# Fewer block pairs at the end of an up projection, and each pair's last product issued one product later

## Chip, cores and metric

The kernel runs on one core of a Trainium2 chip. The metric is the device time of one execution in microseconds (us), lower is better; the time of a kernel is the median of its runs.

## What is computed

Two residual layers on 512 tokens of width 1024, in float32. Each has a token mixer, a cross attention into 256 memory tokens, and a squared-ReLU MLP, every sub-layer followed by a layer norm. The change lies in the MLP, which is run twice, once in each layer:

```python
def sq_relu_mlp(x, w1, b1, w2, b2):          # x 512x1024, w1 1024x4096, w2 4096x1024
    return jnp.square(jax.nn.relu(x @ w1 + b1)) @ w2 + b2
...
x = layer_norm(ALPHA * x + sq_relu_mlp(x, mlp_w1[i], mlp_b1[i], mlp_w2[i], mlp_b2[i]),
               ln_g[i, 2], ln_b[i, 2])
```

## The kernel before

**Number format.** Every float32 operand is split into a high part h and a low part l of a type that TensorE takes at full rate: ScalarE (ACT) casts the high part, VectorE (DVE) subtracts it from the raw value for the low part. A product is then three matmuls: h by h, l by h, h by l (`mm3`, lines 198 to 200 are its three matmuls). So each 128x1024 tile of weights costs one ScalarE cast and one VectorE subtraction before TensorE may read it. The split weights lie in two pools of five buffers each, `wh` and `wl`; a buffer is free again when its last matmul has run.

**The MLP.** The 4096 hidden features are worked in four quarters q of 1024, eight tiles of 128 features each. Quarters 0 to 2 go through `up_down`, quarter 3 through plain products. In `up_down` the up projection makes the hidden values `s`, two buffers of four tiles; the down projection then multiplies them by the quarter of w2 with Strassen's scheme, seven block products (`product`, 24 matmuls of 512 columns each) instead of eight.

**The up projection** takes the eight tiles in four pairs, m = 0, 2, 4, 6. A plain pair is two calls of `feat_tile`, 24 matmuls of 512 columns each, and an evacuation `ev` by ScalarE (Relu and Square, lines 915 and 916). A block pair (`up_pair`) is seven products of 12 matmuls of 256 columns: its VectorE forms sums of weight blocks (lines 869 to 873, buffers of pool `rawd`, six of them), four splits follow (`ub`, `utb`, `uta` of 1024 columns, `ud` of 512; lines 864 and 865), and the seven products are added up by evacuations on both engines (lines 888 to 900). The first, second and the last product belong to `ub`, `ub` and `utb`; the last is `prod(pa, t4, block(1, 1), False)`, copied at line 900 and followed by Relu and Square of both tiles (lines 902 and 903). Which pairs are block pairs stands in `STRASSEN_UP`: none in quarter 0, pairs 1, 2, 3 of quarter 1, all four of quarter 2.

**The start of the down projection.** The first product, into the PSUM banks `u`, needs block a11 of `s` (split by `first_blocks`, line 778 and 779, as soon as the first four tiles are there) and block b11 of w2 (`weight_split`, lines 787 and 788, two halves). The second product, into `f`, needs

- t1, a sum of weight blocks. It is made in place: once b11 is split, GpSimd (POOL) issues a DMA that adds another block of w2 onto the same buffer (`onto_w`, line 968, one per half), and the sum is then split, `t101h` and `t101l` in quarter 1 of layer 0;
- q1, the split of a21 - a22 (line 974, then lines 778 and 779, `q101h`), for which all eight tiles must be done.

A third block sum, t3, is made in the same way from buffers `t`.

**Order.** A planner decides the order of the instructions on each engine before the kernel runs. It goes by program order, but lets a later instruction go ahead of an earlier one when, by its own estimate of durations, the earlier is not ready. On the chip each engine then runs its list in that order, and waits at whatever comes next.

Of the kernel before, what the change touches and what calls it, by code (L numbers as in the profile page):

```python
# [11 lines left out]
AF = mybir.ActivationFunctionType  # L12
# [21 lines left out]
SUM = sum(SEG)  # L34
WU = 1024
LN_T = 7.2
STRASSEN_UP = ((), (1, 2, 3), (0, 1, 2, 3))


def f32(ap):  # L40
    return ap.bitcast(F32)
# [3 lines left out]
def trunk(ctx: ExitStack, tc: tile.TileContext, a: dict, out: bass.AP):  # L45
    nc = tc.nc
    V, A, G, T = nc.vector, nc.scalar, nc.gpsimd, nc.tensor
# [43 lines left out]
    def ld(dst, src):  # L91
        nc.sync.dma_start(dst, src)

    def const_tile(name, shape):
        t = const.tile(shape, F32, name=name)
        ld(t, a[name])
        return t
# [83 lines left out]
    def chain(us, step, fns):  # L181
        for n, fn in enumerate(fns):
            defer(us + step * n, fn)
# [32 lines left out]
    def hf_cols(hf):  # L216
        return slice(hf * 512, (hf + 1) * 512)
# [266 lines left out]
    b1 = const_tile("b1", [P, DEPTH, DFF // P])  # L484
# [169 lines left out]
    for i in range(DEPTH):  # L654
# [147 lines left out]
        def block(r, c):  # L802

            return xm.half(c, slice(256 * r, 256 * r + 256))

        def x_sums():
# [42 lines left out]

            chain(3, 5, [start, q3, q1, q2, q4, end])  # L850

        def up_pair(q, m, n, s):


            src = [a["w1"][i, 8 * q + m + z] for z in range(2)]
            h2 = slice(0, 512), slice(512, 1024)
            u1, u2 = [raw_p.tile([P, WU], F32, tag="raw", name=f"up{n}{m + z}") for z in range(2)]
            ld(u1, src[0])
            ld(u2, src[1])
            ta, tb = [scoped["rawd"].tile([P, WU], F32, tag="rawd", name=f"ut{n}{m}{z}") for z in "ab"]  # L860

            def hl(name, r):
                h, l = [p.tile([P, WU], F32R, tag=t, name=f"{name}{n}{m}{t}")[:, : r.shape[1]] for p, t in ((wh_p, "wh"), (wl_p, "wl"))]
                A.copy(h, r)
                V.tensor_tensor(l, r, f32(h), ALU.subtract)
                return [tuple(z[:, c].rearrange("p (k m) -> p k m", m=P) for z in (h, l)) for c in h2[: r.shape[1] // 512]]

            b11, b21 = hl("ub", u1)
            V.tensor_tensor(ta[:, h2[0]], u1[:, h2[0]], u2[:, h2[0]], ALU.add)
            V.tensor_tensor(tb[:, h2[0]], ta[:, h2[0]], u2[:, h2[1]], ALU.add)  # L870
            V.tensor_tensor(tb[:, h2[1]], tb[:, h2[0]], u1[:, h2[1]], ALU.add)
            t2_, t4 = hl("utb", tb)
            V.tensor_tensor(ta[:, h2[1]], u2[:, h2[0]], u2[:, h2[1]], ALU.add)
            t1, t3 = hl("uta", ta)
            (b22,) = hl("ud", u2[:, h2[1]])

            pa = acc_p.tile([P, 512], F32, tag="acc", name=f"ua{n}{m}")[:, :256]
            pb = acc_p.tile([P, 512], F32, tag="acc", name=f"ub{n}{m}")[:, :256]
            pc = aux_p.tile([P, 512], F32, tag="aux", name=f"uc{n}{m}")[:, :256]
            z1, z2 = s[:, m % 4], s[:, m % 4 + 1]  # L880
            lo, hi = slice(0, 256), slice(256, 512)

            def prod(ps, w, x_, start):
                for k in range(4):
                    mm3(ps, (w[0][:, k], w[1][:, k]), (x_[0][:, k], x_[1][:, k]), start=start and k == 0, stop=k == 3, skip=not start)

            prod(pa, b11, block(0, 0), True)
            A.copy(z1[:, lo], pa)
            prod(pc, b21, block(0, 1), True)
            V.tensor_tensor(z1[:, lo], z1[:, lo], pc, ALU.add)  # L890
            prod(pa, t2_, xq["q2"], False)
            A.activation(z2[:, lo], pa, AF.Copy, scale=-1.0)
            prod(pb, t1, xq["q1"], True)
            A.copy(z2[:, hi], pb)
            prod(pa, t3, xq["q3"], False)
            V.tensor_tensor(z2[:, hi], z2[:, hi], pa, ALU.subtract)
            prod(pb, b22, xq["q4"], False)
            V.tensor_tensor(z2[:, lo], z2[:, lo], pb, ALU.add)  # L898
            prod(pa, t4, block(1, 1), False)
            A.copy(z1[:, hi], pa)  # L900
            for c, z in enumerate((z1, z2)):
                A.activation(z, z, AF.Relu, bias=b1[:, i, 8 * q + m + c : 8 * q + m + c + 1], scale=1.0)  # L902
                A.activation(z, z, AF.Square)

        def up_down(q, n):

            s = [act_p.tile([P, 4, S], F32, tag="act", name=f"s{n}{b}") for b in range(2)]

            def ev(m, ps):
                r = t2(f"r{n}{m}")
                A.activation(r, ps, AF.Relu, bias=b1[:, i, 8 * q + m : 8 * q + m + 1], scale=1.0)
                A.activation(s[m // 4][:, m % 4], r, AF.Square)

            first = 0
            if q == 0:
                feat_first(f"h{n}", 4, lambda m: a["w1"][i, m], xm, ev)  # L920
                first = 4
                assert not later
                b2 = raw_p.tile([P, D], F32, tag="raw", name=f"b2{i}")
                ld(b2, a["b2"][i : i + 1, :].broadcast_to([P, D]))
                for t in range(NT):
                    V.scalar_tensor_tensor(x[t], x[t], ALPHA, b2, ALU.mult, ALU.add)
            a11, a21 = s[0][:, :, :256], s[0][:, :, 256:]
            a12, a22 = s[1][:, :, :256], s[1][:, :, 256:]
            L, R = {}, {}

            def load(name, hf, j):
                z = [scoped["rawd"].tile([P, WU], F32, tag="rawd", name=f"{name}{n}{z}") for z in range(2)]
                for w in range(2):
                    ld(z[w], a["w2"][i, q, hf, j + w])
                return z

            def first_blocks():
                L["M1"] = split(f"a11{n}", a11)
                V.tensor_tensor(a11, a11, a21, ALU.subtract)
                L["M7"] = split(f"q3{n}", a11)  # L940

            if q == 0:
                first_blocks()
                x_sums()
            for m in range(first, KC, 2):
                if m // 2 in STRASSEN_UP[q]:
                    up_pair(q, m, n, s[m // 4])
                else:
                    for z in range(2):
                        ev(m + z, feat_tile(f"h{n}{m + z}", a["w1"][i, 8 * q + m + z], xm, aux_p, "aux"))  # L950
                if m == 2:
                    first_blocks()

            def onto(row, hf, op=ALU.add):
                def evac(g, ps):
                    z = x[2 * row + g][:, hf_cols(hf)]
                    V.tensor_tensor(z, z, ps, op)

                return evac

            def banks(name, p, tag):
                return [p.tile([P, 512], F32, tag=tag, name=f"{name}{n}{g}") for g in range(2)]

            u, f, m2 = banks("u", acc_p, "acc"), banks("f", acc_p, "acc"), banks("m2", tmp_p, "tmp")
            def onto_w(z, hf, j):

                for w in range(2):
                    G.dma_start(z[w], a["w2"][i, q, hf, j + w], accum_op=ALU.add)  # L968

            b = load("b11", 0, 0)  # L970
            w = weight_split(f"b11{n}", b)
            onto_w(b, 1, 0)
            product(u, L["M1"], w, True, onto(0, 0))
            V.tensor_tensor(a21, a21, a22, ALU.subtract)
            w = weight_split(f"t1{n}", b)
            onto_w(b, 1, 2)
            product(f, split(f"q1{n}", a21), w, True, onto(1, 1))
            b21 = load("b21", 0, 2)
            l12 = split(f"a12{n}", a12)
            product(m2, l12, weight_split(f"b21{n}", b21), True, onto(0, 0))  # L980
            t3 = load("t3", 1, 0)
            onto_w(t3, 1, 2)
            V.scalar_tensor_tensor(a11, a11, -1.0, a22, ALU.mult, ALU.subtract)
            w = weight_split(f"t2{n}", b)
            onto_w(b, 0, 2)
            product(u, split(f"q2{n}", a11), w, False, onto(0, 1, ALU.subtract))
            product(u, L["M7"], weight_split(f"t3{n}", t3), False, onto(1, 1, ALU.subtract))
            b22 = load("b22", 1, 2)
            V.tensor_tensor(a12, a12, a11, ALU.add)
            product(f, split(f"q4{n}", a12), weight_split(f"b22{n}", b22), False, onto(0, 1))  # L990
            product(u, split(f"a22{n}", a22), weight_split(f"t4{n}", b), False, onto(1, 0))
# [113 lines left out]
```

## Time and profile before

| | us |
|---|---|
| median of 3 runs | 1243.29 |
| lowest to highest run | 1242.1 to 1243.35 |
| profiled execution, its own time | 1241.42 |
| its span, first to last instruction | 1239.7 |
| TensorE busy | 1191.8 (96%) |
| VectorE busy | 857.7 (69%) |
| ScalarE busy | 617.9 (50%) |

The span is that of the profiled execution, from the first to the last instruction; the time of that execution is 1.7 us longer. A busy share of 96% leaves some 48 us in which TensorE had no matmul running. The granted clock of TensorE is 0.981 of full speed on average. The page of the profile has the span in 40 slices; to find where the idle time lies one asks the trace for TensorE's waits, and then for the order of time around each.

### The profile page before, as it was taken

The numbers are of one execution on the slowest core, as the hardware profiler recorded it, in microseconds if no ns is written. First come the engines' busy times: TensorE is split into PE (matmuls) and PEld (weight loads), VectorE is DVE, ScalarE is ACT, GpSimd is POOL, SyncE is SP. The second block draws the span as 40 slices with busy tenths as digits, with TensorE's granted clock in tenths as the row PEclk, the third lists the DMA queues.
The fourth block names the chain that finished last, engine by engine and source line by source line (L and its number), as shares of the span: only waits on it lengthen the run. The fifth ranks groups of instructions, "written<-read, shape, count | busy, mean of one in ns | idle before, by whom it ended". The sixth has DMA issues, their size and how long they took to land.

```text
span 1239.7 us, 16808 instructions
## 1 busy us (share of the span) xinstructions
PE 1191.8 (96%) x6609; PEld 1035.7 (84%) x6609; DVE 857.7 (69%) x1191; ACT 617.9 (50%) x924; POOL 62.1 (5%) x99
## 2 busy tenths in 40 slices
PE   9999999999999999799799999999999979979997
PEld 7888898898889789689688889988988968968886
DVE  6673575575567996597585599866889659758336
ACT  6585864135324646446446443652464554644430
POOL 0221000000000100100100000000010010010000
PEclk9999999999999999899899999999999989989999
DMA  8253258433255535835745455626453482583411
GB/s 277 77 143 108 86 189 294 146 103 102 82 156 154 102 85 168 172 68 175 165 114 194 127 185 195 192 86 186 139 117 79 158 175 65 181 177 85 119 52 68
DMA packets 50976, 171.85 MB, mean 139 GB/s; under 512 B 6336, under 2 KB 6604, under 8 KB 50896
## 3 DMA queue, kind: packets, MB, share of 16 engines
q1 hardware_dynamic: 42960, 142.96, 35.8%
q0 software_dynamic: 7936, 27.81, 12.5%
q8 instruction: 52, 0.85, 0.3%
q14 instruction: 28, 0.23, 0.1%
HBM read 164.43 MB, written 6.31 MB: 138 GB/s over the span
## 4 chain that ended last, share of the span: by engine, by line
PE 79%; DVE 9%; DMA 5%; ACT 4%; issue 2%; SPq 0%; DVEq 0%; ACTq 0%
PE h L198 5%; PE h L199 5%; PE h L200 5%; PE m L199 3%; PE m L198 3%; PE m L200 3%; DMA b<-in_w 3%; PE u L198 2%; PE u L199 2%; PE u L200 2%; PE ao L198 2%; PE ao L200 2%; PE ao L199 2%; PE q L198 2%; PE q L199 2%; PE q L200 2%
## 5 line engine op out<-in xcount | busy, mean ns | idle before, releaser
L162 DVE TENSOR_TENSOR wl<-raw,wh 128x1024 fp32r<-128x1024 f32 x147 | 179.1, 1220 | 145.9 <-ACT wh L161 143.9
L161 ACT CAST wh<-raw 128x1024 fp32r<-128x1024 f32 x147 | 153.7, 1049 | 226.3 <-PE h L199 52.4
L968 POOL DMA_DIRECT2D b<-in_w x36 | 31.7, 882 | 282.4 <-DVE b1100l L788 62.7
L968 POOL DMA_DIRECT2D t<-in_w x12 | 11.5, 996 | 680.0 <-DMA t<-in_w 451.2
L249 ACT ACTIVATE rs<-mv,eps_t 128x1 f32<-128x1 f32 x24 | 7.1, 295 | 53.2 <-DVE mv L247 53.2
L198 PE MATMUL h<-xm10h,wh 128*128 128x512 f32 (+1 forms) x88 | 31.0, 352 | 0.0
L198 PE MATMUL h<-xm00h,wh 128*128 128x512 f32 (+1 forms) x88 | 31.0, 352 | 0.0
L198 PE MATMUL h<-xm01h,wh 128*128 128x512 f32 (+1 forms) x88 | 31.0, 352 | 0.0
L198 PE MATMUL h<-xm11h,wh 128*128 128x512 f32 (+1 forms) x88 | 31.0, 352 | 0.0
L199 PE MATMUL h<-xm00l,wh 128*128 128x512 f32 (+1 forms) x88 | 30.9, 352 | 0.0
L199 PE MATMUL h<-xm10l,wh 128*128 128x512 f32 (+1 forms) x88 | 30.9, 351 | 0.0
L200 PE MATMUL h<-xm00h,wl 128*128 128x512 f32 (+1 forms) x88 | 30.8, 350 | 0.0
L200 PE MATMUL h<-xm01h,wl 128*128 128x512 f32 (+1 forms) x88 | 30.8, 350 | 0.0
L200 PE MATMUL h<-xm10h,wl 128*128 128x512 f32 (+1 forms) x88 | 30.8, 350 | 0.0
L200 PE MATMUL h<-xm11h,wl 128*128 128x512 f32 (+1 forms) x88 | 30.8, 350 | 0.0
L199 PE MATMUL h<-xm01l,wh 128*128 128x512 f32 (+1 forms) x88 | 30.8, 350 | 0.0
L199 PE MATMUL h<-xm11l,wh 128*128 128x512 f32 (+1 forms) x88 | 30.8, 350 | 0.0
L677 ACT ACTIVATE pr<-s,nm 128x256 f32<-128x256 f32 x32 | 14.9, 471 | 10.4 <-DVE nm L672 7.6
L902 ACT ACTIVATE s<-s,b 128x512 f32<-128x512 f32 x28 | 18.9, 718 | 2.0 <-DVE s L898 2.0
L199 PEld LDWEIGHTS h<-xm10l,wh 128*128 128x128 f32 x88 | 16.7, 189 | 2.3
L199 PEld LDWEIGHTS h<-xm00l,wh 128*128 128x128 f32 x88 | 16.7, 189 | 2.2
L198 PEld LDWEIGHTS h<-xm00h,wh 128*128 128x128 f32 x88 | 16.7, 189 | 2.2
(1696 smaller groups left out, 4259.3 us busy)
## 6 DMA issues: line engine op xcount, KB each, us to landing
raw<-in_w SPq DMA_DIRECT2D x60, 512.0 KB, 3.8
b<-in_w SPq DMA_DIRECT2D x36, 512.0 KB, 4.5
b<-in_w POOLq DMA_DIRECT2D x36, 512.0 KB, 5.7
up<-in_w SPq DMA_DIRECT2D x28, 512.0 KB, 3.7
raw<-in_w_q SPq DMA_DIRECT2D x24, 512.0 KB, 4.1
raw<-in_w_ao SPq DMA_DIRECT2D x16, 512.0 KB, 3.7
t<-in_w SPq DMA_DIRECT2D x12, 512.0 KB, 3.8
t<-in_w POOLq DMA_DIRECT2D x12, 512.0 KB, 9.8
```

Of the source, the lines that this page charges most:

```text
L161: A.copy(h, r)
L162: V.tensor_tensor(l, r, f32(h), ALU.subtract)
L198: T.matmul(out_, l[0], r[0], start=start, stop=False, skip_group_check=skip)
L199: T.matmul(out_, l[0], r[1], start=False, stop=False, skip_group_check=skip)
L200: T.matmul(out_, l[1], r[0], start=False, stop=stop, skip_group_check=skip)
L249: A.activation(rs, mv[:, 1:2], AF.Sqrt, bias=eps_t, scale=1.0)
L677: A.activation(pr[:, ms], ps[:, ms], AF.Exp, bias=nm[:, t_ : t_ + 1], scale=1.0, accum_out=sm[:, t_ : t_ + 1])
L902: A.activation(z, z, AF.Relu, bias=b1[:, i, 8 * q + m + c : 8 * q + m + c + 1], scale=1.0)
L968: G.dma_start(z[w], a["w2"][i, q, hf, j + w], accum_op=ALU.add)
```

## The change

In quarters 1 and 2 of each layer the first three pairs are block pairs and the last is plain. So quarter 1 keeps three block pairs and has the plain one last instead of first, and quarter 2 has three in place of four. The last product of a block pair, with its copy and the Relu and Square of the pair, is kept back and issued behind the first product of the next block pair, or behind the first plain tile that follows. `first_blocks` is called after the third pair instead of the second, where the first pairs are block pairs.

```diff
-STRASSEN_UP = ((), (1, 2, 3), (0, 1, 2, 3))
+STRASSEN_UP = ((), (0, 1, 2), (0, 1, 2))
...
+        open_pairs = []
+
+        def last_product():
+
+            while open_pairs:
+                open_pairs.pop()()
+
...
             prod(pa, b11, block(0, 0), True)
             A.copy(z1[:, lo], pa)
+            last_product()
             prod(pc, b21, block(0, 1), True)
...
-            prod(pa, t4, block(1, 1), False)
-            A.copy(z1[:, hi], pa)
-            for c, z in enumerate((z1, z2)):
-                A.activation(z, z, AF.Relu, bias=b1[:, i, 8 * q + m + c : 8 * q + m + c + 1], scale=1.0)
-                A.activation(z, z, AF.Square)
+
+            def last():
+                prod(pa, t4, block(1, 1), False)
+                A.copy(z1[:, hi], pa)
+                for c, z in enumerate((z1, z2)):
+                    A.activation(z, z, AF.Relu, bias=b1[:, i, 8 * q + m + c : 8 * q + m + c + 1], scale=1.0)
+                    A.activation(z, z, AF.Square)
+
+            open_pairs.append(last)
...
                     for z in range(2):
                         ev(m + z, feat_tile(f"h{n}{m + z}", a["w1"][i, 8 * q + m + z], xm, aux_p, "aux"))
-                if m == 2:
+                        last_product()
+                if m == 4 and first == 0:
                     first_blocks()
```

## Rows read from the trace of the kernel before

**Rows 1.** The page: span and busy time of each engine.

```profile
span 1239.7 us, 16808 instructions
PE 1191.8 (96%) x6609; PEld 1035.7 (84%) x6609; DVE 857.7 (69%) x1191; ACT 617.9 (50%) x924; POOL 62.1 (5%) x99
```

**Rows 2.** TensorE's waits: line waiting, releaser, us in total, times, longest.

```profile
PE f L198 <- ACT q111h L778: 8.5, 1, 8.5
PE f L198 <- ACT q112h L778: 8.1, 1, 8.1
PE f L198 <- ACT q102h L778: 8.0, 1, 8.0
PE f L198 <- ACT q101h L778: 7.9, 1, 7.9
PE ua L198 <- DVE s L896: 1.9, 4, 0.8
...
PE f L198 <- ACT q100h L778: 0.7, 1, 0.7
...
PE f L200 <- DVE q100l L779: 0.5, 1, 0.5
```

**Rows 3.** TensorE in order of time: start, us, [idle before <- releaser].

```profile
506.38 0.28 PE L200 MATMUL ua<-xm01h,utb016wl 128*128 128x256 f32 x1
...
519.53 0.80 PE L198 MATMUL f<-t101h,q101h 128*128 128x512 f32 x1 [7.86 <-ACT q101h L778]
...
520.56 0.63 PE L198 MATMUL f<-t101h,q101h 128*128 128x512 f32 x1
```

**Rows 4.** Granted clock (column after POOL) for 12 us from each resumption.

```profile
519.53:531.53 12.00, 11.99 (x43) 9.75 (x44) 10.48 (x12) 4.80 (x5) 1.76 (x2) 0.80 0.55 138
610.92:622.92 12.00, 12.00 (x41) 9.75 (x42) 10.13 (x12) 4.79 (x5) 1.76 (x2) 0.77 0.51 126
1018.65:1030.65 12.00, 12.00 (x45) 9.76 (x46) 10.82 (x12) 5.01 (x6) 1.75 (x2) 0.83 0.55 135
1109.21:1121.21 12.00, 12.00 (x41) 9.69 (x42) 10.08 (x12) 4.79 (x5) 1.77 (x2) 0.77 0.49 130
```

**Rows 5.** ScalarE in order of time around the first stall, layer 0, quarter 1.

```profile
496.01 1.05 ACT L787 CAST b1101h<-b 128x1024 fp32r<-128x1024 f32 x1 [0.39 <-PE ua L199]
...
499.76 1.05 ACT L787 CAST b1101h<-b 128x1024 fp32r<-128x1024 f32 x1
...
513.07 1.04 ACT L787 CAST t101h<-b 128x1024 fp32r<-128x1024 f32 x1 [3.30 <-DMA b<-in_w]
514.02 0.37 ACT L900 COPY s<-ua 128x256 f32<-128x256 f32 x1
514.28 1.33 ACT L902 ACTIVATE s<-s,b 128x512 f32<-128x512 f32 x2
...
518.44 1.04 ACT L778 CAST q101h<-s 128x1024 fp32r<-128x1024 f32 x1
```

**Rows 6.** VectorE in the same stretch.

```profile
500.85 1.23 DVE L788 TENSOR_TENSOR b1101l<-b,b1101h 128x1024 fp32r<-128x1024 f32 x1 [0.53 <-ACT b1101h L787]
...
516.69 1.23 DVE L974 TENSOR_TENSOR s<-s,s 128x1024 f32<-128x1024 f32 x1 [0.72 <-ACT s L903]
```

**Rows 7.** GpSimd's accumulating transfers in the same stretch: start, us, queue line.

```profile
497.46 0.88 POOL L968 DMA_DIRECT2D t<-in_w  x1 [56.88 <-DVE s L898]
...
505.15 0.88 POOL L968 DMA_DIRECT2D b<-in_w  x1 [4.24 <-DVE s L896]
```

**Rows 8.** Stretches: PE, PEld, DVE, ACT, POOL busy us (instructions), clock, DMA share, GB/s.

```profile
475.20:485.30 10.10, 10.10 (x85) 10.06 (x84) 7.00 (x10) 6.00 (x9) 0.00 (x0) 1.00 0.57 208
464.30:475.20 10.90, 10.90 (x49) 9.03 (x49) 6.65 (x9) 3.84 (x5) 0.00 (x0) 1.00 0.35 98
425.00:435.00 10.00, 8.76 (x38) 6.59 (x37) 9.97 (x11) 7.46 (x9) 0.00 (x0) 1.00 0.59 116
540.00:550.00 10.00, 10.00 (x46) 8.26 (x45) 9.82 (x13) 2.81 (x4) 0.00 (x0) 1.00 0.01 2
```

## Prediction

> **What bounds the kernel now.** I read the page first, then TensorE's waits, then the order of time around the longest of them. The page says that TensorE is busy for 1191.8 of 1239.7 us [rows 1]: this kernel is bound by TensorE, so only its 48 idle us, its slow stretches and its number of matmuls can move the time. TensorE's waits put most of the idle time in four places of one kind: the matmuls into `f` wait for the cast of q1, 8.5, 8.1, 8.0 and 7.9 us, together 32.5 us [rows 2]. They are quarters 1 and 2 of both layers, exactly the quarters that end in a block pair. Quarter 0, whose last pairs are plain, loses 0.7 and 0.5 us at the same place, 1.2 in all, in each layer [rows 2].
>
> The order of time shows why. The last matmul of the up projection starts at 506.38 and `f` only at 519.53 [rows 3]; in between there is the first down product, some 5 us, and then nothing. ScalarE has the second cast of t1 ahead of the copy that ends the last block pair. That cast waits for an accumulating DMA and starts at 513.07; only behind it come the copy (514.02), the Relus (514.28) and Squares, although the product that they wait for was there at 506.7 [rows 3, 5]. Then VectorE forms a21 - a22 at 516.69 [rows 6], ScalarE casts q1 at 518.44 [rows 5], and TensorE goes on. The DMA is late for its part: b11's second half was cast at 499.76 and its low part done at 502.08, but the transfer onto it was issued at 505.15 [rows 5 to 7], 7.7 us after the first of a row of four accumulating transfers, at 497.46 [rows 7]; the fourth seems to wait until the first has landed.
>
> The stall has a second price. TensorE comes back at half clock: the granted clock is 0.80, 0.77, 0.83 and 0.77 over the 12 us from each resumption [rows 4], while in quarter 0, where the stall was 1.2 us, it stayed at 1.00 [rows 8]. [...]
>
> **The change, part by part.** Durations are from the profiled execution, 1241.4 us, of which 1239.7 are span; the median of the runs is 1243.3, so the sum is made on the first and carried over to the median as a difference.
>
> *More matmul work.* Each layer has one block pair fewer (quarter 1 keeps three, quarter 2 goes from four to three). A block pair of 84 matmuls takes 10.1 us, a plain pair of 48 takes 10.9 [rows 8]. Twice 0.8: **+1.6 us**. It all lies on TensorE, so it counts in full.
>
> *The last pair plain.* What f needs is (a) t1 and (b) q1. For both I follow the buffers of `wh` back from the end E of the last up matmul. Now: pair 6 takes four of the five, b11's first half gets the one that pair 4's last product frees (cast at 496.01, E - 10.6), the second one of pair 6's (499.76, E - 6.9) [rows 5]. After: pair 4 starts at E - 22.4 (10.1 for six own products and pair 2's last, 5.45 for each tile, 1.44 for pair 4's last product between them). The buffers come free 2.9, 4.3, 8.6 and 10.1 us into pair 4; the first two go to the two plain tiles, the next two to b11, so E - 13.8 and E - 12.3. The second half is 5.4 us earlier. From its cast to the start of f the trace has 519.53 - 499.76 = 19.8 us [rows 3, 5]. If every step of that chain kept its length, f would start at E + 7.5, against E + 5.4 where the first down product ends: 2.1 us of stall. Two steps should shorten. The buffers of t3 are no longer needed for a fourth pair's sums, so its two transfers can go first and be out of the way (up to 3 us); and the evacuation of pair 4 now runs during tile 7, 5 us before E, so behind the last tile there are only one Relu and one Square of half the work, against the copy and four passes at 514.02 [rows 5]. Then TensorE is the later one and the stall is 0. The bounds are therefore 0 and 2.1; quarter 0's 1.2, with VectorE at 9.97 of 10 us [rows 8], is the nearest row, but its VectorE also made the sums of x, so I take 0.7. The four stalls: **-32.5 + 2.8 us**. With stalls below quarter 0's the clock should stay up as it did there: **-10.0 us**.
>
> *The last product behind the next pair's first.* Within block pairs TensorE waits four times for line 896, which must empty bank `pa` before the last product may write it: 1.9 us [rows 2]. One product of 1.44 us in between covers the longest, 0.8: **-1.9 us**. Against it stands that `utb` is held through the next pair's first product, so that four buffers of the running pair and this one fill `wh`. The next pair's `ub` then gets its buffer 2.9 us into the running pair, which is 7.2 before it is needed; a cast and a subtraction take 1.05 and 1.23 [rows 5, 6]. Covered; without that cover it is 2.3 us for each of the twelve pairs that follow a block pair, the plain ones counted too. The PSUM banks just suffice: two pairs of `pa` and `pb` are the four of that pool.
>
> *Block pair at the head of quarter 1.* Its preparation (6 to 7 us of VectorE) falls into quarter 0's down products. Quarter 2 has had this arrangement: at 540 to 550 VectorE is busy for 9.82 of 10 us and TensorE for 10.00 [rows 8]. So nothing, or a few tenths. The same row covers the loss of slack when TensorE no longer pauses before f, as quarter 0's down products run without a pause too. *first_blocks later*: two casts and three VectorE passes (some 2.1 and 3.7 us) move from pair 4 to the plain tiles, where VectorE has 2.4 us of other work in 10.9; hidden. Nothing is moved on SP or GpSimd but what follows from free buffers.
>
> Sum: 1.6 - 32.5 + 2.8 - 10.0 - 1.9 = **-40.0 us**. The profiled time goes from 1241.4 to 1201.4, the median from 1243.3 to **1203.3 us**.
>
> [...] In the trace the copy at 514.02 ran behind a cast that waited for a DMA, though its own product was 7 us old [rows 3, 5]. [...]
>
> **The rivals.**
>
> *The queue still blocks (1222 us).* The planner took the accumulating transfer for quicker than it is: it put t1's cast ahead of the copy, and the cast then waited. After the change t1's first cast may use tile 6's buffer at E - 6.9 and be placed ahead of pair 4's copy. If the transfer lands at E or later, copy, four passes, tile 7's own and q1 follow. F is then late by 2.1 us (the chain at its full length) to 5.2 (if the last transfer waits another 3.1 us for its turn, as it did from 502.08 to 505.15 [rows 6, 7]). For it: nothing in the edit keeps t1's cast from going ahead. Against: quarter 0, where the same cast came with a plain tail, lost only 1.2. With 3.5 in place of 0.7 us, and the clock falling or not (the trace has no stall between 1.2 and 7.9): 1203.3 + 11.2 + 0 to 10 = 1214.5 to 1224.5.
>
> *Slower (1246 us): b11 gets the held buffer.* If b11's second half is split only in the buffer that pair 4's put-off last product frees, at E - 5.4, the chain of 19.8 us ends at E + 14.4 and the stall is 9.0, not 8.1: 3.6 us more over four places, no clock gained, +1.6 for the matmuls, -1.9 for the bank: +3.3, so 1246.6. The point from which the stall stays is a cast at E - 6.9, as now. For it: the planner's choice of buffers can't be read from the trace. Against: two others are free 5 us sooner.
>
> *It doesn't do what it says (1205 us).* The order is the planner's. If it places the put-off product back ahead of the next pair's first, the 1.9 us stay [rows 2] and the rest is as forecast.
>
> **How the numbers follow.** Forecast, with the 1205 case in it: 0.65, 1200 to 1208 (stall 0 to 1.9 us in each place). Queue still blocks: 0.22, 1208 to 1226. Little or no gain, 0.05, around 1243. Slower: 0.06. Some 0.02 for what I don't see. Range: leaving out the last three, 1199 to 1226. About 0.2% (2.5 us) is what a measurement of this kernel can tell from no change. Faster 0.88, same 0.05, slower 0.07.
>
> **What would show it.** Right: the four waits of f for q1 below 2 us, the granted clock at 1.00 through the down products, no waits of `ua` on line 896, TensorE's matmuls 72 fewer, its idle time near 12 us. The chain: b11's second cast 12 us before the end of the up projection, t1's casts done before u ends. Wrong: a wait of f above 2 us with ScalarE idle ahead of a cast of t1 (first rival), or b11's second cast later than 7 us before the end (second); new waits at the first matmul of a pair would mean that the held buffer is not covered.

## The result, and the profile after

| | before | changed |
|---|---|---|
| median, us | 1242.69 | 1207.64 |
| lowest to highest run | 1240.72 to 1243.35 | 1203.98 to 1210.54 |
| profiled execution, its own time | 1241.42 | 1205.39 |
| its span | 1239.7 | 1203.5 |

The ratio of the times is 0.9719, with a 95% interval of 0.9685 to 0.9753: 35 us faster, where 40 were forecast. The runs of the changed kernel lie further apart (6.6 us) than those before (2.6).

The page of the changed kernel, against rows 1: 72 matmuls fewer, and 19 us idle in place of 48.

```profile
span 1203.5 us, 16624 instructions
PE 1184.3 (98%) x6537; PEld 1027.5 (85%) x6537; DVE 847.3 (70%) x1173; ACT 616.2 (51%) x912; POOL 61.1 (5%) x99
```

TensorE's waits in the changed kernel (line waiting, releaser, total, times, longest), against rows 2:

```profile
PE f L198 <- ACT q112h L778: 2.3, 1, 2.3
...
PE f L198 <- ACT q101h L778: 0.6, 1, 0.6
PE f L200 <- DVE q112l L779: 0.6, 1, 0.6
PE f L200 <- DVE q111l L779: 0.6, 1, 0.6
PE f L200 <- DVE q101l L779: 0.6, 1, 0.6
PE f L200 <- DVE q102l L779: 0.6, 1, 0.6
PE f L198 <- ACT q111h L778: 0.6, 1, 0.6
...
PE f L198 <- ACT q102h L778: 0.4, 1, 0.4
```

The four waits of 8 us have become four pairs of short ones: for the high part of q1 0.4 to 2.3, and then 0.6 for its low part, 6.3 us in all in place of 32.5. The wait of `ua` on line 896 is gone from the list. The clock, in 12 us from each resumption, against rows 4:

```profile
512.15:524.15 12.00, 11.40 (x49) 9.12 (x50) 11.90 (x13) 6.90 (x7) 1.75 (x2) 1.00 0.59 136
...
1073.18:1085.18 12.00, 11.40 (x42) 8.93 (x43) 10.40 (x12) 5.84 (x6) 1.76 (x2) 0.86 0.44 104
```

It stays at 1.00 but for the last place, where the wait was longest; there the missing share is 0.14 of 12 us, 1.7 us.

ScalarE in order of time around the first place, layer 0, quarter 1, against rows 5:

```profile
492.20 1.05 ACT L787 CAST b1101h<-b 128x1024 fp32r<-128x1024 f32 x1 [0.74 <-PE ua L199]
493.64 1.05 ACT L787 CAST b1101h<-b 128x1024 fp32r<-128x1024 f32 x1 [0.39 <-PE ub L199]
...
501.86 1.05 ACT L787 CAST t101h<-b 128x1024 fp32r<-128x1024 f32 x1 [4.93 <-DMA b<-in_w]
502.82 0.68 ACT L927 ACTIVATE r<-h,b 128x512 f32<-128x512 f32 x1
504.31 1.05 ACT L787 CAST t101h<-b 128x1024 fp32r<-128x1024 f32 x1 [0.82 <-DMA b<-in_w]
...
505.80 0.35 ACT L910 COPY s<-ua 128x256 f32<-128x256 f32 x1
506.19 0.72 ACT L912 ACTIVATE s<-s,b 128x512 f32<-128x512 f32 x1
...
507.48 1.03 ACT L787 CAST b2101h<-b 128x1024 fp32r<-128x1024 f32 x1
508.42 0.68 ACT L927 ACTIVATE r<-h,b 128x512 f32<-128x512 f32 x1
...
511.06 1.05 ACT L778 CAST q101h<-s 128x1024 fp32r<-128x1024 f32 x1 [1.29 <-DVE s L987]
```

TensorE begins the first down product at 505.93 here. So b11 is cast 13.7 and 12.3 us before the end of the up projection, as was worked out (13.8 and 12.3), and nearly the same in the other three places. But the casts of t1 still stand in ScalarE's list ahead of work that is ready: 4.93 us of standing still for the first transfer (in about the last half of it tile 6's product is there already), and behind it tile 6's Relu and Square (lines 927, 928), then the put-off copy, Relu and Square of the third pair (lines 910 to 913). The last tile's Relu, ready at 506, runs at 508.42. The accumulating transfers:

```profile
486.64 0.87 POOL L981 DMA_DIRECT2D t<-in_w  x1 [46.02 <-DMA t<-in_w]
489.50 0.90 POOL L981 DMA_DIRECT2D t<-in_w  x1 [1.98 <-DMA up<-in_w]
495.82 0.89 POOL L981 DMA_DIRECT2D b<-in_w  x1 [5.43 <-DVE b1101l L788]
496.96 0.87 POOL L981 DMA_DIRECT2D b<-in_w  x1 [0.25 <-issue]
```

The two onto t3 now go first, and the two onto b11 leave as soon as its low parts are done; the fourth no longer waits its turn as in rows 7. In three of the four places t1's second transfer lands 7.1 to 7.3 us after its issue, 1.7 to 1.9 us before the first down product begins. In the fourth (layer 1, quarter 2) it takes 8.9 us, though it leaves just as far ahead of that product and 1.1 us behind the first as in the others, and lands at 1065.27, when that product begins (1065.30). There ScalarE stands still for 2.75 us ahead of its cast, with tile 6's Square and the put-off copy ready behind it:

```profile
1065.34 1.05 ACT L787 CAST t112h<-b 128x1024 fp32r<-128x1024 f32 x1 [2.75 <-DMA b<-in_w]
...
1066.83 0.35 ACT L910 COPY s<-ua 128x256 f32<-128x256 f32 x1
```

This is the place of the wait of 2.3 us and of the fall of the clock. Why this one transfer took longer, the trace doesn't show.

### The profile page after: what moved, and what is told of

The parts are those of the page before. It is cut to its first block, busy times and chain, and to the rows that moved or that the text cites. A ratio compares the mean times of both kernels' runs of the same rounds, so it can differ in the third digit from the quotient of the medians.

```text
span 1203.5 us, 16624 instructions
## 1 busy us (share of the span) xinstructions
PE 1184.3 (98%) x6537; PEld 1027.5 (85%) x6537; DVE 847.3 (70%) x1173; ACT 616.2 (51%) x912; POOL 61.1 (5%) x99
## 4 chain that ended last, share of the span: by engine, by line
PE 82%; DVE 7%; DMA 4%; ACT 3%; issue 3%; POOL 0%; DVEq 0%; POOLq 0%; ACTq 0%; SPq 0%
PE h L198 5%; PE h L199 5%; PE h L200 5%; PE m L198 3%; PE m L199 3%; PE m L200 3%; PE u L198 3%; PE u L199 3%; PE u L200 3%; PE ao L200 2%; PE ao L198 2%; PE ao L199 2%; PE f L200 2%; PE q L199 2%; PE q L198 2%
## 5 line engine op out<-in xcount | busy, mean ns | idle before, releaser
L162 DVE TENSOR_TENSOR wl<-raw,wh 128x1024 fp32r<-128x1024 f32 x151 | 184.1, 1221 | 152.5 <-ACT wh L161 150.4
L161 ACT CAST wh<-raw 128x1024 fp32r<-128x1024 f32 x151 | 157.9, 1048 | 220.6 <-PE h L199 51.8
L198 PE MATMUL h<-xm00h,wh 128*128 128x512 f32 (+1 forms) x96 | 34.2, 356 | 0.0
L198 PE MATMUL h<-xm10h,wh 128*128 128x512 f32 (+1 forms) x96 | 34.2, 356 | 0.0
L199 PE MATMUL h<-xm10l,wh 128*128 128x512 f32 (+1 forms) x96 | 34.1, 355 | 0.0
L199 PE MATMUL h<-xm00l,wh 128*128 128x512 f32 (+1 forms) x96 | 34.1, 355 | 0.0
L198 PEld LDWEIGHTS h<-xm01h,wh 128*128 128x128 f32 x96 | 18.2, 189 | 2.5
L200 PEld LDWEIGHTS h<-xm00h,wl 128*128 128x128 f32 x96 | 18.2, 189 | 2.5
L199 PEld LDWEIGHTS h<-xm11l,wh 128*128 128x128 f32 x96 | 18.2, 189 | 2.5
L200 PEld LDWEIGHTS h<-xm10h,wl 128*128 128x128 f32 x96 | 18.1, 189 | 2.5
```

The costliest lines, as they stand in the source:

```text
L198: T.matmul(out_, l[0], r[0], start=start, stop=False, skip_group_check=skip)
L199: T.matmul(out_, l[0], r[1], start=False, stop=False, skip_group_check=skip)
L200: T.matmul(out_, l[1], r[0], start=False, stop=stop, skip_group_check=skip)
```

## The experiments

**Which half of the change it is.** The theory: the plain last pair gives nearly all, the put-off product 1.9 us. The rival: each is needed for the other.

```diff
-STRASSEN_UP = ((), (1, 2, 3), (0, 1, 2, 3))
+STRASSEN_UP = ((), (0, 1, 2), (0, 1, 2))
```

> The kernel before, with block pairs 0, 1, 2 in quarters 1 and 2, but no product put off. Theory (the plain last pair is the gain): the four waits of f for q1 are as short as in the changed kernel, 0.4 to 2.5 us, the clock stays at 1.00 but for one or two short falls, and the waits of ua on line 896 (1.9 us in all) come back: 1207.6 + 1.9 = 1209.5 us, between 1206 and 1213. Rival (the put-off product is needed too, since it takes the pair's evacuation away from the end): waits of 4 us or more, clock falls, 1225 us or more.

Measured: 1198.89 us, ratio 0.9642 (0.9628 to 0.9656). Faster than the changed kernel by 8.7 us, where it was expected 1.9 slower. TensorE has no wait of f left in quarters 1 and 2, and one of 0.3 us on line 896. ScalarE at the same place:

```profile
496.30 0.37 ACT L900 COPY s<-ua 128x256 f32<-128x256 f32 x1
496.70 1.34 ACT L902 ACTIVATE s<-s,b 128x512 f32<-128x512 f32 x2
497.95 1.14 ACT L903 ACTIVATE s<-s 128x512 f32<-128x512 f32 x2
501.85 1.05 ACT L787 CAST t101h<-b 128x1024 fp32r<-128x1024 f32 x1 [2.76 <-DMA b<-in_w]
502.80 0.68 ACT L915 ACTIVATE r<-h,b 128x512 f32<-128x512 f32 x1
504.36 1.05 ACT L787 CAST t101h<-b 128x1024 fp32r<-128x1024 f32 x1 [0.88 <-DMA b<-in_w]
...
506.75 1.05 ACT L787 CAST b2101h<-b 128x1024 fp32r<-128x1024 f32 x1 [0.81 <-PE h L199]
507.71 0.68 ACT L915 ACTIVATE r<-h,b 128x512 f32<-128x512 f32 x1
...
510.35 1.05 ACT L778 CAST q101h<-s 128x1024 fp32r<-128x1024 f32 x1 [1.29 <-DVE s L974]
```

Here the up projection ends at 506.78 (first matmul of u), against 505.93 in the changed kernel. The third pair's copy, Relus and Squares ran at 496.3 to 499, in time in which ScalarE of the changed kernel stood still. So the last tile's Relu comes 0.9 us behind the end of the up projection, and in the changed kernel 2.5; the cast of q1 3.6 us behind it, and there 5.1. The first down product takes 5.4 us: with the cast's 1.05 the one is in time and the other is not. The put-off product does shorten the up projection itself: from a quarter's first matmul to u it takes 41.5, 41.2, 41.2 and 41.2 us in the changed kernel, and 42.2, 41.4, 41.7 and 41.2 here, 1.5 us in all. What it gains there it gives back, and more, at f. The clock does not part the two profiled executions: this one lost 1.7 us to a fall as well, in another part of the kernel (at 745.2 us, behind waits of 0.6 and 1.1 us for the matmuls into `po`).

The other half, against the changed kernel:

```diff
-STRASSEN_UP = ((), (0, 1, 2), (0, 1, 2))
+STRASSEN_UP = ((), (1, 2, 3), (0, 1, 2, 3))
...
                 if m == 4 and first == 0:
                     first_blocks()
+            last_product()
```

> The changed kernel's put-off product with the block pairs of the kernel before (1, 2, 3 and 0, 1, 2, 3); the last pair's own last product is issued at the end of the up projection. Theory: the four waits of f stay at 7 to 9 us with the half clock after them, only the 1.9 us of waits on line 896 go: 1241 us, between 1238 and 1244. Rival (the put-off product carries a good part of the gain): waits of f below 5 us, 1225 us or less.

Measured: 1236.27 us, ratio 0.9949 (0.9929 to 0.9969). The waits of f stay:

```profile
PE f L198 <- ACT q101h L778: 9.8, 1, 9.8
...
PE f L198 <- ACT q112h L778: 7.0, 1, 7.0
```

The theory's side, but 6.7 us faster and not 2, and outside the expected 1238 to 1244. The profiled execution (1240.29 us) was the slowest of its four runs, the others took 1234.9 to 1236.3. Their granted clock is 0.984 and 0.985, against 0.980 in the profiled one, so less of the clock was lost in them; where, is not in the trace that there is, and stays open.

**What the 8 us were.** The theory: the late transfer of t1 and what queues behind its cast. The rival: the last block pair's own chain of evacuation, a21 - a22 and the cast of q1.

```diff
             w = weight_split(f"b11{n}", b)
-            onto_w(b, 1, 0)
```

> The kernel before without the DMA that adds the second block onto b11 to make t1 (in all three quarters): t1 is then b11 split a second time, so the output isn't the reference's. Theory (the stall is the late transfer plus what queues behind its cast on ScalarE): the four waits of f fall to under 1.5 us and the clock stays up: 1243 - 32.5 + 4 - 10 = 1204 us, between 1200 and 1211. Rival (the last block pair's copy, Relus, Squares, a21 - a22 and the cast of q1 are too long by themselves): waits of 4 us or more, 1225 us or more.

Measured: 1210.35 us, ratio 0.9737 (0.9722 to 0.9751). TensorE's waits:

```profile
PE f L198 <- ACT q111h L778: 2.2, 1, 2.2
PE f L198 <- ACT q101h L778: 2.2, 1, 2.2
...
PE f L198 <- ACT q102h L778: 0.7, 1, 0.7
...
PE f L198 <- ACT q112h L778: 0.7, 1, 0.7
```

Without the transfer, and with the block pair still last, 8 us become 0.7 to 2.2: most of the stall was the transfer's and what queued behind its cast, and not the evacuation's own length. Two of the four waits are above the expected 1.5; in the one at 514 ScalarE had a cast of t2 ahead of that of q1, and it ran at 512.12, after waiting 0.4 us for its own transfer.

```diff
             t3 = load("t3", 1, 0)
-            onto_w(t3, 1, 2)
```

> The kernel before without the DMA that adds a block onto t3 (two transfers per quarter less; the output isn't the reference's). Theory (the fourth accumulating transfer waits for the first to land): t1's second transfer is issued within 1 us of b11's second low part instead of 3 us behind it, and shares the DMA engines with fewer; the waits of f shrink by 2.5 to 4.5 us each, to 3.5 to 5.5, and the clock still falls: 1243 - 14 = 1229 us, between 1222 and 1234. Rival (the transfer is held by something else than the number under way): the waits stay at 8 us, 1243 us.

Measured: 1225.92 us, ratio 0.9867 (0.9841 to 0.9892). GpSimd's second transfer onto b11, against rows 7:

```profile
502.49 0.88 POOL L968 DMA_DIRECT2D b<-in_w  x1 [2.50 <-DVE b1101l L788]
```

It leaves at 502.49, 0.4 us after b11's second low part (502.09), and not at 505.15. So it was t3's transfers ahead of it that held it. The traces of before and of the changed kernel agree: in neither does GpSimd issue one of its 48 accumulating transfers while three are under way, and the four late ones of the kernel before each leave 0.31 us after an earlier one has landed. The waits of f are 3.8, 6.4, 4.7 and 4.2 us, 13.4 less together, one of them above the expected 5.5; the clock is 0.86, 0.86, 0.86 and 0.77 behind them.

**What is left of the stall in the changed kernel.** The theory: ScalarE's list. So the two casts go to VectorE, and nothing else is changed:

```diff
-        def weight_split(name, src):
+        def weight_split(name, src, cast=A.copy):
...
-                A.copy(h, r)
+                cast(h, r)
...
-            w = weight_split(f"t1{n}", b)
+            w = weight_split(f"t1{n}", b, V.tensor_copy)
```

> The changed kernel with t1's two high parts cast on VectorE instead of ScalarE. Theory (what is left of the stall is tile 6's and pair 4's evacuation queued on ScalarE behind casts of t1 that wait for the transfer): the waits of f in quarters 1 and 2 fall from 6.3 us in all to under 2.5, no clock fall there: 1200 us, between 1197 and 1203. Rival (the same wait on VectorE, ahead of a21 - a22 in its list): f still waits 1 us or more in each place, 1205 to 1210 us.

Measured: 1196.73 us, ratio 0.9635 (0.9621 to 0.9650). One wait of 0.6 us is left in quarters 1 and 2. ScalarE goes on as soon as a product is there:

```profile
498.34 0.69 ACT L927 ACTIVATE r<-h,b 128x512 f32<-128x512 f32 x1 [2.29 <-PE h L200]
...
499.77 0.37 ACT L910 COPY s<-ua 128x256 f32<-128x256 f32 x1
...
505.97 0.68 ACT L927 ACTIVATE r<-h,b 128x512 f32<-128x512 f32 x1
```

VectorE now stands still instead (4.57 us ahead of the first cast), and TensorE does not wait for it: what comes next in VectorE's list was not ready earlier.

```profile
501.36 0.69 DVE L787 CAST t101h<-b 128x1024 fp32r<-128x1024 f32 x1 [4.57 <-DMA b<-in_w]
```

**Only the third pair at once.** The put-off product should cost only where its evacuation meets a cast of t1.

```diff
                 if m == 4 and first == 0:
+                    last_product()
                     first_blocks()
```

> The changed kernel, but the third pair's last product is issued at once, ahead of the plain tiles; the first two pairs still put theirs off. Theory (the put-off product costs only where its evacuation falls behind a cast of t1): no waits of f in quarters 1 and 2, no waits on line 896 in the first pairs: 1198.5 us, between 1195 and 1201. Rival (holding the utb buffers, or the later first_blocks, is what costs): 1204 us or more, with waits elsewhere.

Measured: 1201.56 us, ratio 0.9674 (0.9659 to 0.9688): 6.1 us faster than the changed kernel, so most of its loss is the third pair's put-off product (the intervals of the two ratios just touch); but 3 us short of the expected. Waits of f of 0.9 and 1.5 us are left, and 0.6 for the low part in three places. The two longer ones are the places where t1's second transfer landed late, 0.5 us before the first down product began and 0.1 us after it had begun. In the first of them it took 8.5 us:

```profile
497.58 0.87 POOL L982 DMA_DIRECT2D b<-in_w  x1 [0.25 <-issue]
...
506.15 1.05 ACT L787 CAST t101h<-b 128x1024 fp32r<-128x1024 f32 x1 [1.59 <-DMA b<-in_w]
```

At the same place it took 7.3 us in the changed kernel, 5.7 in the one with no product put off, and 8.0 in the next one, which puts none off either; no run here shows what makes the difference. Where it landed equally early, 1.7 us before the down product, f waits 0.6 us here and 1.0 to 1.2 in the changed kernel.

**The place of first_blocks**, in the kernel with the plain last pair and nothing put off:

```diff
-                if m == 2:
+                if m == 4 and first == 0:
                     first_blocks()
```

> Plain last pair without putting off, with first_blocks behind the third pair as in the changed kernel (it stood behind the second where this order ran at 1198.9 us). Theory (its place doesn't matter, VectorE and ScalarE have room during the plain tiles): 1199 us, between 1197 and 1201. Rival (its casts and passes move ahead of b11's split and make t1 later): 1203 us or more, waits of f of 0.5 us or more.

Measured: 1199.84 us (1197.4 to 1200.33), ratio 0.9657 (0.9642 to 0.9671), with one wait of f of 0.5 and 0.6 us. Against 1198.89 (1197.75 to 1199.49) no difference that these runs can tell. This kernel differs from the changed one by the put-off product alone, so that product costs 7.8 us.

**b11 earlier** in the changed kernel: its load, split and the transfers onto it are written ahead of the last tile (`b11_split` holds the three lines that are taken out below).

```diff
                     for z in range(2):
+                        if m == 6 and z == 1:
+                            b11_split()
                         ev(m + z, feat_tile(...))
...
-            b = load("b11", 0, 0)
-            w = weight_split(f"b11{n}", b)
-            onto_w(b, 1, 0)
+            b, w = R["b"]
```

> The changed kernel with b11's load, split and the transfers onto it written ahead of the last plain tile instead of behind it, so that b11's first half takes the buffer that tile 7 had and is cast 4 us earlier, the second half 1 us earlier. ScalarE's list otherwise stays as it is, casts of t1 ahead of tile 6's evacuation. Theory (only the landing against the place in the list counts): t1's transfers land before ScalarE comes to them or less than 1 us after, the waits of f in quarters 1 and 2 fall from 6.3 us to under 3 in all, 1201 us, between 1198 and 1204. Rival (the list itself is too long for the time that is left behind the last tile): f waits as before, 1205 to 1210 us.

Measured: 1203.25 us, ratio 0.9690 (0.9676 to 0.9703). Within the expected time, but not for the expected reason: the waits of f fall only from 6.3 to 5.1 us in all, and it is the long one of 2.3 and the fall of the clock that are gone. The interval of the ratio overlaps that of the changed kernel (0.9685 to 0.9753), so a gain is likely but not shown.

```profile
491.16 0.89 POOL L957 DMA_DIRECT2D b<-in_w  x1 [0.68 <-DVE b1101l L788]
495.86 0.87 POOL L957 DMA_DIRECT2D b<-in_w  x1 [3.82 <-DVE b1101l L788]
...
504.21 1.05 ACT L787 CAST t101h<-b 128x1024 fp32r<-128x1024 f32 x1 [2.17 <-DMA b<-in_w]
```

The transfers left 4.7 and 1.1 us earlier, and the second landed when it did before (504.13 against 504.24): it took 8.3 us in place of 7.3, and the first 9.2 in place of 6.0. Here an earlier issue alone didn't bring the data sooner; why, no run shows.

**Another order of the down products**, on the kernel with the plain last pair and nothing put off: a12 by b21 second, q1 by t1 third.

```diff
+            b21 = load("b21", 0, 2)
+            l12 = split(f"a12{n}", a12)
+            product(m2, l12, weight_split(f"b21{n}", b21), True, onto(0, 0))
             V.tensor_tensor(a21, a21, a22, ALU.subtract)
             w = weight_split(f"t1{n}", b)
...
-            b21 = load("b21", 0, 2)
-            l12 = split(f"a12{n}", a12)
-            product(m2, l12, weight_split(f"b21{n}", b21), True, onto(0, 0))
```

> Plain last pair without putting off, and the down products in another order: a12 by b21 second, q1 by t1 third, so that f has a product more of time (5.4 us). Theory: the 1.2 us at f in quarter 0 of both layers go too, nothing new waits: 1198.9 - 2.5 = 1196.4 us, between 1194 and 1198.5. Rival (b21's or a12's split is now the late one, or t2's cast, which waits for its own transfer): a wait of 1 us or more at m or u, 1199 us or more.

Measured: 1201.7 us, ratio 0.9676 (0.9659 to 0.9692): slower than without. The rival's side, by a mechanism that it had not named. The M7 product (q3 by t3) goes into the banks `u` again, and waits until VectorE has read the product before it out of them:

```profile
PE u L198 <- DVE xp L957: 2.2, 2, 1.1
PE u L198 <- DVE xin L957: 1.4, 2, 0.7
```

And quarter 0's waits at f do not go: 1.0 and 0.7 us of 1.2 are left.

**The two best edits together**, the plain last pair with nothing put off and t1's casts on VectorE (`weight_split` gets its `cast` as above):

```diff
-STRASSEN_UP = ((), (1, 2, 3), (0, 1, 2, 3))
+STRASSEN_UP = ((), (0, 1, 2), (0, 1, 2))
...
-            w = weight_split(f"t1{n}", b)
+            w = weight_split(f"t1{n}", b, V.tensor_copy)
```

> Plain last pair, no product put off, t1's high parts cast on VectorE: the two best edits together. Without waits of f left in quarters 1 and 2 (none at 1198.9 us) only quarter 0's 1.2 us at f in each layer and what lies outside can go: 1197 us, between 1195 and 1199. If putting off has a use of its own once nothing queues behind t1's casts, it is slower than the 1196.7 us of the kernel with both.

Measured: 1199.22 us (1196.79 to 1202.46), ratio 0.9656 (0.9638 to 0.9675). No gain over either alone that these runs can tell. Its profiled execution still has a wait of f of 0.8 us in layer 0, quarter 1, and 0.6 and 0.4 us for the low part, where none were expected; in that first place t1's second transfer landed 0.9 us after the first down product had begun. Whether putting off has a use of its own once ScalarE is free stays open: 1196.7 with it, 1199.2 without, in runs that overlap.

## Why the prediction was right, and where it wasn't

**What bound the kernel.** Right. The waits of f and the half clock behind them (in the first place a granted 0.50 for the 4 us from 519.53, and 1.00 again from 524.53) were most of the time that could be gained. That the transfer and the queue behind its cast made most of the 8 us, and not the pair's own evacuation, is shown by leaving the transfer out (0.7 to 2.2 us left); that the fourth transfer waited for those under way, by leaving t3's out.

**More matmul work, +1.6.** 72 matmuls fewer, as counted. No run has the time by itself; but three up projections of the changed kernel take 41.2 us, which is three block pairs of 10.1 and a plain one of 10.9. In the plain pair of rows 8 the matmuls of the split type, 512 columns each, start 0.227 us apart at a granted 1.00 (24 in 5.44 us from 468.66), 0.44 ns a column; three float32 ones of 144 columns in the same kernel (line 623, from 714.27) take 0.64 us, 1.5 ns a column.

**The last pair plain, -29.7.** The mechanism is right to a tenth of a microsecond up to the transfers (b11 cast 13.7 and 12.3 us ahead of the end). The rest of the stall was mis-sized: 0.7 us in each place was assumed; 1.2, 1.0, 1.2 and 2.9 were measured (in order of time), 6.3 in all, so -26.2. The step that failed is the sentence that the third pair's evacuation runs during tile 7 and leaves one Relu and one Square behind the last tile. It was queued behind t1's casts and ran at 505.80 to 507.6, after the end of the up projection. That is the first rival's mechanism. In three places it came at a lower price than its 2.1 to 5.2 us, since the transfers landed 4.1 to 4.4 and 1.7 to 1.9 us before the up projection ended and not after it. In the fourth the second transfer landed at that end, the rival's own condition, and the 2.9 us are its price. A late landing alone does not cost that much: with t1's casts on VectorE, in layer 0, quarter 1, it also came only 0.1 us before the end, and f waited 0.6 us. That the casts ahead of it in ScalarE's list held the evacuation back shows when they are taken out of that list: tile 6's Relu ran 6.7 us ahead of the end of the up projection (498.34, u from 505.04) and not 3.1 (502.82, u from 505.93), and the put-off copy 5.3 ahead and not 0.1.

**The clock, -10.0.** The 10.0 us were the author's estimate, the missing share of the 12 us in each line of rows 4; no run shows this term as a time of its own. What the trace of before shows is that matmuls of 512 columns start 0.43 us apart while the granted clock is 0.50 (520.56 to 523.54), and 0.23 apart at 1.00 (525.28 to 527.78). By the same estimate the term was mis-sized by the one fall that remained: -8.3 in the profiled execution. Its two slower runs, 1208 us of span, have a mean granted clock of 0.994 and 0.995, against 0.996 in the two faster ones; so they lost a little more of it. Which place it was in them is not known; a late transfer, as in the fourth place, may be the cause, but only one execution has a trace.

**The put-off product, -1.9.** Wrong as a sum. Its waits on line 896 did go, and the up projections are 1.5 us shorter for it. But most of the 1.9 us went with the plain last pair already: without putting off, line 896 costs 0.3 us there (0.6 with first_blocks behind the third pair). And the step named nothing that it delays, while it delays q1; only the first rival had a price for it. With the put-off product the kernel takes 1207.6 us, without it 1199.8, first_blocks in the same place. Of these 7.8 us, 6.1 are the third pair's (1207.6 against 1201.6 when that one is issued at once). In the profiled executions the waits of f in quarters 1 and 2 are 6.3 us with it and 1.1 without. That the held `utb` buffer is covered was right: no first matmul of a pair waits.

**The sum.** Of the -40.0 us, the profiled execution shows -36.0: +1.6, -26.2, -8.3 and -1.9 make -34.8, and 1.2 us are not assigned. The median is 4.3 us above the forecast; in the profiled execution, 4.0 above its own, the terms of the stall and its clock are 5.2 short. So the median lies in the forecast's case (1200 to 1208) by 0.4 us, and two of the four runs lie above it; the case's condition, a stall of at most 1.9 us in each place, failed in the fourth.

**Head of quarter 1, first_blocks.** Right: no wait at the start of quarter 1, and the place of first_blocks makes no difference (1199.8 against 1198.9).

**The rivals.** "Slower, b11 gets the held buffer" didn't happen: both halves had the two earlier buffers. "It doesn't do what it says" neither. The first rival is the one that holds in part, and the range reached into it for that reason. Its sign, a wait of f above 2 us with ScalarE idle ahead of a cast of t1, is there in one place of four. The idle time "near 12 us", named as a sign of being right, was a slip: the forecast's own terms leave 47.9 - 29.7 - 1.9 = 16.3 us, and 19.2 were measured.

## What to carry to other kernels

Where a planner with its own durations writes an in-order list, look for casts that wait for a transfer and ask what is behind them: work that is ready must stand ahead, or the cast must go to an engine that has nothing else to do. Putting work off to win a small wait early on puts its evacuation later too; cost it at the place where it lands, not where it leaves. And before a change of two halves is costed, see whether the wait that one half removes is still there after the other.

## What was not expected of the hardware

The clock doesn't follow the length of a single wait. With t1's transfer left out, two waits of f of 2.2 us were followed by a granted clock of 1.00 and 0.86:

```profile
514.17:526.17 12.00, 12.00 (x52) 9.78 (x53) 11.88 (x12) 5.72 (x6) 1.75 (x2) 1.00 0.66 155
...
996.65:1008.65 12.00, 12.00 (x46) 9.68 (x47) 10.80 (x11) 4.56 (x5) 1.78 (x2) 0.86 0.58 138
```

Each of the twelve waits of 3.8 us or more had a fall in it or just behind it: the four of 7.9 to 8.5 us in the kernel before (0.77 to 0.83, rows 4), the four of 7.0 to 9.8 us in the one with the put-off product alone (matmuls of 512 columns 0.43 us apart for 4.3 us behind each, and then 0.23), and the four of 3.8 to 6.4 us in the one without t3's transfers (0.77 to 0.86). And a cast of 1024 columns to the split type takes 0.69 us on VectorE, where ScalarE needs 1.05.
